# Differential values projected 512 columns wide, gates of two groups in every other stage

## The chip, the cores and the metric

The kernel runs on one core of a Trainium2 chip. The metric is the device time of one execution in microseconds (us); shorter is better.

## The reference, cut to what matters

Two layers (`DEPTH = 2`) over 512 frames of width 2048, all in float32. In each layer one input projection feeds three things: differential attention (8 heads, two softmax maps each), latent attention (8 heads, "MLA") and a SiLU gate. Then comes one output projection.

```python
for l in range(DEPTH):
    h = _rmsnorm(x, norm_g[l])
    proj = jnp.einsum('bsd,de->bse', h, w_in[l])
    dq, dk, dv, cq, ckv, kr, gate = jnp.split(proj, offs, axis=-1)
    ...
    o_a = _diff_attention(dq[:, :, 0], dq[:, :, 1], dk[:, :, 0], dk[:, :, 1], dv, lam, rel_bias)
    ...
    o_b = _mla_attention(q_nope, q_rope, k_nope, k_rope, v_b)
    ...
    y = jnp.concatenate([o_a, o_b], axis=-1) * jax.nn.silu(gate)
    x = x + jnp.einsum('bse,ed->bsd', y, w_out[l])
return _rmsnorm(x, final_norm_g)
```

The change touches `dv` (the values of the differential heads, 1024 columns of `w_in`), the first 1024 columns of `gate`, and where the values of both attentions are kept.

## The kernel before

**Weights.** They are read in units of at most 128 x 1024 elements (`in_units`, `plan`). `emit_dma` loads a unit to `raw`; `emit_split` makes of it a rounded part `whi` on ScalarE (L195) and a remainder `wlo` on VectorE (L196). Activations are kept as such pairs too. A product is three matmuls (`mm3`, L249): high by high, low by high, high by low. Four pairs of `whi` and `wlo` are in use at a time, and the split runs two units ahead of the unit in work.

**Groups.** `group` makes the pieces of one projection: for each unit, for each of `nb` output blocks, one piece. The outer loop is over units, so all `nb` blocks accumulate at once, each in a PSUM bank of its own, from a pool `pj` of four. When a block has had its last piece, `evac` copies it out, and the bank goes to the next group that asks. `mm_T` holds the weight still and streams 512 frames (moving operand 512 wide, output transposed); `mm_S` holds the activation still and streams the weight columns, so that its matmuls are as wide as the unit.

**Stages.** In each layer TensorE works through CQ (four blocks, `mm_S`, 512 wide), then four stages `i` = 0 to 3, one for each pair of differential heads, then a last stage with gates and CKV, then the output projection and MLA. Stage `i` has

- G (only from `i` = 1 on): the gates of pair `i-1`, 2 blocks, 4 units of 4 k-blocks, `mm_T`: pieces of 12 matmuls;
- V: the values of pair `i`, 4 blocks, 4 units of 4 k-blocks by 256 columns, `mm_S`: pieces of 12 matmuls, 256 wide;
- QK: queries and keys of pair `i`, 4 blocks, 8 units of 2 k-blocks, `mm_T`: pieces of 6 matmuls.

The last stage has G of pair 3, then the gates of MLA (GM, two groups of 4 blocks with pieces of 6 matmuls), then CKV.

**Evacuation.** The four blocks of QK are evacuated by `evac_qk`: blocks 0 and 1 (queries) take two copies on ScalarE and two subtractions on VectorE (L486) each; blocks 2 and 3 (keys) take four copies on ScalarE (L99) and four subtractions on VectorE (`kl`, L746) each, which read the bank until their end. A block of V takes one copy, on ScalarE or VectorE in turn (L751); a block of gates an exponential and a copy on ScalarE, while its reciprocals and its product (L719, L720, L724) are put into a list, `later`, that `run_later` spreads over the pieces that follow.

**Attention.** The attention of pair `i-1` is cut into items (`diff_items`): scores, softmax, transposes (L309), product with the values (L573), norm, and the product with the gate (L592). `mix` lays them between the pieces of stage `i` by the pieces' costs, from a share `MIX_DIFF` of the stage on to its end. So each engine's order is written out by the program; the engines meet by semaphores, and each works through its own list in order.

Of the kernel before, what the change touches and what calls it, by code (L numbers as in the profile page):

```python
# [11 lines left out]
F32 = mybir.dt.float32  # L12
# [5 lines left out]
P = 128  # L18
S = 512
NSB = S // P  # L20
# [21 lines left out]
MLAG = (0, 2, 3, 4)  # L42
PACE = 1.365
SQ_DVE = (0, 2)
EDGE = ((11, 13, 19, 21), (17, 23, 25, 28))
MIX_NORM = (-0.11, 0.63)
MIX_DIFF = (0.08, 1.0)
# [7 lines left out]
def tile_hybrid_trunk(ctx, tc, x, norm_g, w_in, diff_lambda, diff_subln_g, mla_q_norm_g,  # L55
                      mla_w_q_b, mla_kv_norm_g, mla_w_kv_b, w_out, rel_bias, final_norm_g,
                      onehot, cos2, sin1, out):
    nc = tc.nc
# [4 lines left out]
    def pool(name, bufs, space=None):  # L63
        kw = {} if space is None else {"space": space}
        return ctx.enter_context(tc.tile_pool(name=name, bufs=bufs, **kw))
# [3 lines left out]
    rawp = pool("raw", RAW)  # L69
    whip = pool("whi", BUFS)  # L70
    wlop = pool("wlo", BUFS)
    vp = pool("v", 2)
    smp = pool("sm", 4)
    ptp = pool("pt", 2)
    bip = pool("bias", 2)
# [10 lines left out]
    def B(shape, dtype, name):  # L86
        return big.tile(shape, dtype, tag="B", name=name)
# [20 lines left out]
    def in_units(l, cols, nk):  # L108
        w = sum(c for _, c in cols)
        ids = []  # L110
        for k0 in range(0, KD, nk):
            n = min(nk, KD - k0)
            srcs, off = [], 0
            for c0, cw in cols:
                srcs.append((off, cw, w_in[l, k0 * P:(k0 + n) * P, c0:c0 + cw].rearrange("(k p) c -> p k c", p=P)))
                off += cw
            ids.append((add_unit(srcs, n, w), k0, n))
        return ids
# [31 lines left out]
    for l in range(DEPTH):  # L150
        g = {}
        g["CQ"] = in_units(l, [(O_CQ, QL)], 2)
        for i in range(4):
            if i:
                g["G", i - 1] = in_units(l, [(O_GATE + (i - 1) * 256, 256)], 4)
            g["V", i] = in_units(l, [(O_DV + i * 256, 256)], 4)
            g["QK", i] = in_units(l, [(O_DQ + i * 256, 256), (O_DK + i * 256, 256)], 2)
        g["G", 3] = in_units(l, [(O_GATE + 3 * 256, 256)], 4)
        for c in range(2):
            g["GM", c] = in_units(l, [(O_GATE + 1024 + c * 512, 512)], 2)  # L160
        g["CKV"] = in_units(l, [(O_CKV, KVL + ROPE)], 3)
        g["OD", 0] = out_units(l, 0, 0)
        g["QR"] = qr_units(l)
        for j in range(4):
            g["QN", j] = qn_units(l, j)
            g["KV", j] = kv_units(l, j)
            if j:
                g["OD", j] = out_units(l, j, 0)
        for c in range(4):
            g["OM", c] = out_units(l, c, 8)  # L170
        plan.append(g)
# [145 lines left out]
    with tc.manual_schedule():  # L317
# [228 lines left out]
        def diff_items(l, i, qk, v, gate):  # L546
            slots = []
            for hp in range(2):
                h = 2 * i + hp
                o_ = {}  # L550
                for qb in range(NSB):
                    st_ = {}

                    def a(hp=hp, h=h, qb=qb, st_=st_, o_=o_):
                        if qb == 0:
                            if h not in biases:
                                biases[h] = load_bias(h)
                            o_["o"] = T("o", op, "o")
                            o_["ssq"] = stat("ssq")
                            o_["bt"] = biases.pop(h)  # L560
                        if qb == 1 and hp == 0:
                            biases[h + 1] = load_bias(h + 1)
                        diff_scores(l, qk[hp], qb, o_["bt"], st_)
                        if qb == NSB - 1:
                            qk.pop(hp)

                    def b(qb=qb, st_=st_):
                        transpose_p(qb, st_)

                    def c(hp=hp, qb=qb, o_=o_, st_=st_):  # L570
                        bk = bank("ov")
                        for kb in range(qb + 1):
                            nc.tensor.matmul(bk[:, :P], lhsT=st_["pt"][:, kb * P:(kb + 1) * P],  # L573
                                             rhs=v["t"][:, kb, hp * P:(hp + 1) * P], start=kb == 0, stop=kb == qb)
                        acopy(o_["o"][:, qb * P:(qb + 1) * P], bk[:, :P], scale=st_["rc"])
                        nc.scalar.activation(bk[:, :P], bk[:, :P], AF.Square, scale=st_["rc"],
                                             accum_out=o_["ssq"][:, qb:qb + 1])

                    slot = [a, b, c]
                    if qb == NSB - 1:  # L580
                        def d1(o_=o_):
                            rs = stat("ors")
                            rsqrt(rs[:, 0:4], o_["ssq"][:, 0:4], 4, 1.0 / (2 * DH))
                            o3 = o_["o"].rearrange("p (b d) -> p b d", b=NSB)
                            nc.vector.tensor_tensor(o3, o3, rs[:, 0:4].unsqueeze(2).to_broadcast([P, NSB, P]), op=ALU.mult)

                        def d2(h=h, o_=o_):
                            bk = bank("oT")
                            for b in range(NSB):
                                pe_t(bk[:, b * P:(b + 1) * P], o_["o"][:, b * P:(b + 1) * P])  # L590
                            y = gate(h)
                            nc.vector.scalar_tensor_tensor(out=y, in0=bk, scalar=gsub[:, l:l + 1], in1=y, op0=ALU.mult, op1=ALU.mult)  # L592

                        slot += [d1, d2]
                    slots.append(slot)
            return pipeline(slots, DLAG)

        def mla_items(l, j, qk, v, gate, rope):
            slots = []
            for hp in range(2):  # L600
                h = 2 * j + hp
                o_ = {}
                for qb in range(NSB):
                    st_ = {}

                    def a(hp=hp, qb=qb, st_=st_):
                        mla_scores(qk["t"], hp, j, rope, qb, st_)
                        if hp == 1 and qb == NSB - 1:
                            qk.pop("t")
                            if j % 2:  # L610
                                rope.pop(("q", j // 2))

                    def b(qb=qb, st_=st_):
                        transpose_p(qb, st_)

                    def c(hp=hp, qb=qb, o_=o_, st_=st_):
                        if qb == 0:
                            o_["bk"] = bank("oT")
                        for kb in range(qb + 1):
                            nc.tensor.matmul(o_["bk"][:, qb * P:(qb + 1) * P], lhsT=v["t"][:, kb, hp * P:(hp + 1) * P],  # L620
                                             rhs=st_["pt"][:, kb * P:(kb + 1) * P], start=kb == 0, stop=kb == qb)

                    slot = [a, b, c]
                    if qb == NSB - 1:
                        def d(h=h, o_=o_):
                            y = gate(h)
                            nc.vector.tensor_tensor(y, o_.pop("bk"), y, op=ALU.mult)

                        slot.append(d)
                    slots.append(slot)  # L630
            return pipeline(slots, MLAG)
# [9 lines left out]
        for l in range(DEPTH):  # L641
            g = plan[l]
            ah = act_h(l)
# [84 lines left out]

            pend = []
            for i in range(4):  # L730
                qk, v = {}, {}

                def evac_qk(b, bk, qk=qk):
                    if b < 2:
# [10 lines left out]
                        for n in (m, 1 - m):  # L745
                            nc.vector.tensor_tensor(hd["kl"][half(n), m], bk[half(m)], k[half(m), m].bitcast(F32), op=ALU.subtract)  # L746

                def evac_v(b, bk, v=v):
                    if "t" not in v:
                        v["t"] = vp.tile([P, NSB, 256], F32, tag="v", name="v")  # L750
                    (nc.vector.tensor_copy if b % 2 else acopy)(v["t"][:, b, :], bk[:, :256])  # L751

                pieces = []
                if i:
                    pieces += group(g["G", i - 1], 2, mm_T(ah), evac_gate(2 * i - 2))
                pieces += group(g["V", i], NSB, mm_S(ah, 256), evac_v, cost=2)
                pieces += group(g["QK", i], 4, mm_T(ah), evac_qk)
                mix(pieces, pend, MIX_DIFF)
                pend = diff_items(l, i, qk, v, gate_y)
# [7 lines left out]
                    split_pair(gates[h // 4][:, h % 4:h % 4 + 2, :], y[j])  # L767
                return item

            pieces = group(g["G", 3], 2, mm_T(ah), evac_gate(6))  # L770
            for c in range(2):
                pieces += group(g["GM", c], 4, mm_T(ah), evac_gate(8 + 4 * c))
            pieces += group(g["CKV"], NSB, mm_S(ah, KVL + ROPE), evac_ckv, cost=2.6)
# [123 lines left out]
            def mla_proj(j, qk, v):  # L897
# [16 lines left out]
                def kv_piece(b):  # L914
# [16 lines left out]
                    if sb == 3:  # L931
                        finish(u)
                    if "t" not in v:
                        v["t"] = vp.tile([P, NSB, 256], F32, tag="v", name="vm")
                    if sb % 2 == 1:
                        src = banks[0].rearrange("p (b c) -> p b c", b=2)
                        (nc.vector.tensor_copy if sb == 1 else acopy)(v["t"][:, sb - 1:sb + 1, :], src)

                return pieces + [(8 if b < 2 else 4, lambda b=b: kv_piece(b)) for b in range(6)]

            def out_pieces(key, y, evac, ahead=2):
                return group(g[key], NSB, mm_S(act_y(y), 512), evac, ahead=ahead)

            qkv = [({}, {}) for _ in range(4)]
            mix(mla_proj(0, *qkv[0]), even([lambda p=p: qr_T(p) for p in range(4)]), MIX_QR)
            gm = lambda h, gate_y=gate_y: gate_y(8 + h)
            pend = mla_items(l, 0, *qkv[0], gm, rope)
# [123 lines left out]
```

## Time and profile before

| | |
|---|---|
| median of 3 runs | 1766.7 us (1764.92 to 1767.01) |
| the profiled execution | 1766.37 us |
| its span, first to last instruction | 1764.6 us |
| TensorE (PE) busy | 1735.2 us, 98% of the span |
| VectorE (DVE) busy | 970.0 us, 55% |
| ScalarE (ACT) busy | 703.3 us, 40% |
| mean granted TensorE clock | 0.996 |

PE is the matmuls, PEld the loads of their stationary operands. A matmul's busy time reaches into the next one's, since they are pipelined: what one costs is the distance from its start to the next start, and not its own duration. A busy share of PE alone therefore doesn't tell that it runs at its peak.

### The profile page before, as it was taken

The page shows a single profiled execution, that of the slowest core. Times are in us where ns is not written, and L with a number is a line of the kernel's source. Part 1 is how long each engine was busy: PE and PEld are TensorE (multiplying, and loading weights), DVE is VectorE, ACT ScalarE, POOL GpSimd, SP SyncE. Part 2 cuts the span into 40 slices and gives each one's busy share as a digit, 9 for nine tenths or more (in the row PEclk, how much of TensorE's full clock was granted, in tenths as well). Part 3 has the DMA queues.
Part 4 walks back from the last instruction along what each step waited for, and adds up shares of the span by engine and source line. Part 5 has one row for each costly group of instructions (what it writes and reads, how often), then busy time and mean ns, then how long its engine had stood idle before and what let it go on. Part 6 is the DMA issues. An engine that isn't in the chain of part 4 may idle for free.

```text
span 1764.6 us, 23519 instructions
## 1 busy us (share of the span) xinstructions
PE 1735.2 (98%) x9245; PEld 1486.4 (84%) x9245; DVE 970.0 (55%) x1785; ACT 703.3 (40%) x1424; POOL 32.0 (2%) x53
## 2 busy tenths in 40 slices
PE   6999999999999999999999999999999999999997
PEld 4888889898888988888879898888988898888886
DVE  5425646463656774464362263654645676655554
ACT  5324434443443443333362244443543444433433
POOL 1000000000000000000000000000000000000000
PEclk9999999999999999999999999999999999999999
DMA  5552323232332432313333333332324225213223
GB/s 180 163 160 84 96 84 108 72 119 76 105 95 81 123 105 64 120 60 117 122 107 89 92 104 88 96 97 83 108 72 129 75 84 155 72 61 120 84 90 125
DMA packets 142330, 179.34 MB, mean 102 GB/s; under 512 B 16942, under 2 KB 94812, under 8 KB 142092
## 3 DMA queue, kind: packets, MB, share of 16 engines
q1 hardware_dynamic: 142220, 177.85, 33.0%
q8 instruction: 72, 1.18, 0.3%
q14 instruction: 38, 0.31, 0.1%
HBM read 169.39 MB, written 13.67 MB: 104 GB/s over the span
## 4 chain that ended last, share of the span: by engine, by line
PE 97%; ACT 1%; DVE 1%; DMA 1%; issue 0%; POOL 0%; SPq 0%; ACTq 0%; POOLq 0%; DVEq 0%
PE pj L249 84%; PE oT L620 2%; PE ov L573 2%; PE pT L309 2%; PE sc L523 2%; PE sc L493 2%; PE sc L492 2%; PE nT L309 1%; DMA xs<-in_x 1%; PE oT L309 0%; PE cT L309 0%; ACT xn L99 0%; DVE nt L457 0%; ACT whi L195 0%; ACT junk L424 0%
## 5 line engine op out<-in xcount | busy, mean ns | idle before, releaser
L196 DVE TENSOR_TENSOR wlo<-raw,whi 128x1024 fp32r<-128x1024 f32 (+1 forms) x272 | 327.5, 1211 | 298.1 <-ACT whi L195 291.9
L249 PE MATMUL pj<-hThi,whi 128*128 128x512 f32 x1024 | 410.0, 400 | 0.0
L249 PE MATMUL pj<-hThi,wlo 128*128 128x512 f32 x1024 | 400.3, 391 | 0.0
L249 PE MATMUL pj<-hTlo,whi 128*128 128x512 f32 x1024 | 399.3, 390 | 0.0
L195 ACT ACTIVATE whi<-raw 128x1024 fp32r<-128x1024 f32 (+1 forms) x272 | 282.7, 1047 | 182.2 <-PE pj L249 106.3
L249 PE MATMUL pj<-whi,yhl 128*128 128x512 f32 x1024 | 323.8, 397 | 0.0
L249 PE MATMUL pj<-whi,hThi 128*128 128x256 f32 (+2 forms) x768 | 241.4, 314 | 2.1 <-ACT hThi L99 2.1
L249 PE MATMUL pj<-whi,hTlo 128*128 128x256 f32 (+2 forms) x768 | 236.1, 307 | 0.0
L249 PE MATMUL pj<-wlo,hThi 128*128 128x256 f32 (+2 forms) x768 | 235.9, 307 | 0.0
L249 PEld LDWEIGHTS pj<-hThi,wlo 128*128 128x128 f32 x1024 | 192.2, 188 | 41.8
L249 PEld LDWEIGHTS pj<-hThi,whi 128*128 128x128 f32 x1024 | 192.7, 188 | 36.6
L249 PEld LDWEIGHTS pj<-hTlo,whi 128*128 128x128 f32 x1024 | 192.9, 188 | 35.6
L249 PEld LDWEIGHTS pj<-whi,yhl 128*128 128x128 f32 x1024 | 185.5, 188 | 34.0
L249 PE MATMUL pj<-wlo,yhl 128*128 128x512 f32 x512 | 200.6, 392 | 0.0
L509 ACT ACTIVATE s<-s,mx 128x128 f32<-128x128 f32 (+3 forms) x128 | 71.0, 555 | 300.5 <-DVE mx L507 300.5
L249 PEld LDWEIGHTS pj<-whi,hThi 128*128 128x128 f32 x768 | 147.4, 192 | 7.8 <-ACT hThi L99 2.5
L249 PEld LDWEIGHTS pj<-whi,hTlo 128*128 128x128 f32 x768 | 147.2, 192 | 5.7 <-DVE hTlo L462 0.7
L249 PEld LDWEIGHTS pj<-wlo,hThi 128*128 128x128 f32 x768 | 146.9, 191 | 5.4
L249 PEld LDWEIGHTS pj<-wlo,yhl 128*128 128x128 f32 x512 | 96.1, 188 | 21.3
L720 DVE RECIPROCAL ge<-ge 128x256 f32<-128x256 f32 x64 | 112.2, 1753 | 2.2
L503 DVE CUSTOM_DVE_ANT_0 s<-sc,bt 128x128 f32<-128x128 f32 (+3 forms) x128 | 57.1, 483 | 79.4 <-POOL bt L413 54.2
L529 ACT ACTIVATE s<-sc,mx 128x128 f32<-128x128 f32 (+1 forms) x64 | 33.8, 528 | 137.9 <-DVE mx L527 137.9
(153 smaller groups left out, 1870.2 us busy)
## 6 DMA issues: line engine op xcount, KB each, us to landing
raw<-in_w_in SPq DMA_DIRECT2D x112, 512.0 KB, 3.8
raw<-in_w_in SPq DMA_DIRECT2D x128, 256.0 KB, 3.0
raw<-in_w_out SPq DMA_DIRECT2D x64, 512.0 KB, 3.7
xs<-in_x SPq DMA_DIRECT2D x32, 256.0 KB, 5.4
bt<-btab SPq DMA_DIRECT2D x16, 512.0 KB, 5.2
btab<-vecd SPq DMA_DIRECT2D x16, 320.0 KB, 6.2
raw<-in_w_in SPq DMA_DIRECT2D x10, 480.0 KB, 3.7
raw<-in_mla_w_q_b SPq DMA_DIRECT2D x16, 256.0 KB, 3.4
```

Of the source, the lines that this page charges most:

```text
L195: nc.scalar.activation(hi[:, :n], raw[:, :n], AF.Copy)
L196: nc.vector.tensor_tensor(lo[:, :n], raw[:, :n], hi[:, :n].bitcast(F32), op=ALU.subtract)
L249: nc.tensor.matmul(dst, lhsT=a, rhs=b, start=first and t == 0, stop=last and t == 2)
L309: nc.tensor.transpose(dst, src, ident)
L492: nc.tensor.matmul(dst, lhsT=q[:, m], rhs=khi, start=first, stop=False)
L493: nc.tensor.matmul(dst, lhsT=q[:, m], rhs=klo, start=False, stop=True)
L503: nc.vector.tensor_tensor_reduce(out=sm_t[:, :w], in0=bk[:, :w], in1=bt[:, m, 512 - w:512], op0=ALU.add, op1=ALU.max, scale=1.0, scalar=LO ...
L509: nc.scalar.activation(s[m][:, :w], s[m][:, :w], AF.Exp, bias=mx[:, 2 + m:3 + m], accum_out=sm[:, m:m + 1])
L523: nc.tensor.matmul(bk[:, :w], lhsT=qk[:, par, q], rhs=qk[:, 2 + par, :w], start=True, stop=False)
L573: nc.tensor.matmul(bk[:, :P], lhsT=st_["pt"][:, kb * P:(kb + 1) * P], rhs=v["t"][:, kb, hp * P:(hp + 1) * P], start=kb == 0, stop=kb == qb)
L620: nc.tensor.matmul(o_["bk"][:, qb * P:(qb + 1) * P], lhsT=v["t"][:, kb, hp * P:(hp + 1) * P], rhs=st_["pt"][:, kb * P:(kb + 1) * P], start ...
L720: nc.vector.reciprocal(e[:, c], e[:, c])
```

## The change

Values of the differential heads are projected for two pairs of heads at once: the group V exists for `i` = 0 and 2 alone, 512 columns wide, with 8 units of 2 k-blocks. Each of its pieces has 6 matmuls of 512 columns, where before there were 12 of 256. The gates follow a table `GATES`: stage 1 computes the gates of pairs 0 and 1, stage 3 those of pairs 2 and 3, stages 0 and 2 none, and the last stage begins with GM. The tile of values is 128 x 4 x 512: the first of a layer in the pool `v`, which now has one buffer, the second in the pool of big tiles. The values of MLA are kept in one tile with two halves, used by `j % 2`.

```diff
+GATES = ((), (0, 1), (), (2, 3))
...
-    vp = pool("v", 2)
+    vp = pool("v", 1)
...
         for i in range(4):
-            if i:
-                g["G", i - 1] = in_units(l, [(O_GATE + (i - 1) * 256, 256)], 4)
-            g["V", i] = in_units(l, [(O_DV + i * 256, 256)], 4)
+            for n in GATES[i]:
+                g["G", n] = in_units(l, [(O_GATE + n * 256, 256)], 4)
+            if i % 2 == 0:
+                g["V", i] = in_units(l, [(O_DV + i * 256, 512)], 2)
             g["QK", i] = in_units(l, [(O_DQ + i * 256, 256), (O_DK + i * 256, 256)], 2)
-        g["G", 3] = in_units(l, [(O_GATE + 3 * 256, 256)], 4)
...
-                                             rhs=v["t"][:, kb, hp * P:(hp + 1) * P], start=kb == 0, stop=kb == qb)
+                                             rhs=v["t"][:, kb, h % 4 * P:(h % 4 + 1) * P], start=kb == 0, stop=kb == qb)
+                        if h % 4 == 3 and qb == NSB - 1:
+                            v.pop("t")
...
-                    (nc.vector.tensor_copy if b % 2 else acopy)(v["t"][:, b, :], bk[:, :256])
+                        v["t"] = B([P, NSB, 512], F32, "v") if i else vp.tile([P, NSB, 512], F32, tag="v", name="v")
+                    (nc.vector.tensor_copy if b % 2 else acopy)(v["t"][:, b, :], bk)
...
-                if i:
-                    pieces += group(g["G", i - 1], 2, mm_T(ah), evac_gate(2 * i - 2))
-                pieces += group(g["V", i], NSB, mm_S(ah, 256), evac_v, cost=2)
+                for n in GATES[i]:
+                    pieces += group(g["G", n], 2, mm_T(ah), evac_gate(2 * n))
+                if i % 2 == 0:
+                    pieces += group(g["V", i], NSB, mm_S(ah, 512), evac_v)
                 pieces += group(g["QK", i], 4, mm_T(ah), evac_qk)
...
-            pieces = group(g["G", 3], 2, mm_T(ah), evac_gate(6))
+            pieces = []
```

How the order of instructions moves is seen on PE at three places. Each row is an instruction: line, operation, what it writes and reads (with the tiles' numbers), size, and the engines whose semaphores it waits for. A `pj` tile is one block's bank; `oT` are transposes of the attention of the pair before.

The first place is the start of V in stage 0 of the first layer, after the last matmul of CQ. Before:

```order
L249 MATMUL pj_453<-wlo_614,hThi_410 128x512
L249 MATMUL pj_699<-whi_645,hThi_167 128x256 [waits Activation_49]
L249 MATMUL pj_699<-whi_645,hTlo_168 128x256
L249 MATMUL pj_699<-wlo_646,hThi_167 128x256 [waits DVE_49]
...
L249 MATMUL pj_712<-whi_645,hThi_167 128x256 [waits DVE_49]
```

And now:

```order
L250 MATMUL pj_453<-whi_613,hTlo_411 128x512
L250 MATMUL pj_453<-wlo_614,hThi_410 128x512
L250 MATMUL pj_698<-whi_645,hThi_167 128x512 [waits Activation_49]
L250 MATMUL pj_698<-whi_645,hTlo_168 128x512
L250 MATMUL pj_698<-wlo_646,hThi_167 128x512 [waits DVE_49]
...
L250 MATMUL pj_705<-whi_645,hThi_167 128x512 [waits DVE_49]
```

The matmuls are twice as wide; a piece has 6 of them in place of 12, so that the second block (`pj_712`, `pj_705`) comes after 6.

The second place is the step from stage 1 to stage 2, between the last piece of QK (`pj_1758` before, `pj_1692` now, block 3) and what follows. Before, G of pair 1 follows:

```order
L309 MATMUL oT_2088<-ident_110,o_1636 128x128 [waits Activation_49] x2
L249 MATMUL pj_1758<-hThi_410,whi_1962 128x512
...
L249 MATMUL pj_2115<-hThi_167,whi_2011 128x512 [waits DVE_49,PE_49,Activation_49]
...
L249 MATMUL pj_2128<-hThi_167,whi_2011 128x512 [waits DVE_49,PE_49]
...
L249 MATMUL pj_2115<-hThi_176,whi_2045 128x512 [waits Activation_49]
```

Now V of pairs 2 and 3 follows:

```order
L310 MATMUL oT_2025<-ident_110,o_1589 128x128 [waits Activation_49] x2
L250 MATMUL pj_1692<-hThi_410,whi_1899 128x512
...
L250 MATMUL pj_2052<-whi_1948,hThi_167 128x512 [waits DVE_49,PE_49,Activation_49]
...
L250 MATMUL pj_2059<-whi_1948,hThi_167 128x512 [waits DVE_49,PE_49]
...
L250 MATMUL pj_2066<-whi_1948,hThi_167 128x512 [waits DVE_49,PE_49]
...
L250 MATMUL pj_2073<-whi_1948,hThi_167 128x512 [waits DVE_49,PE_49]
...
L250 MATMUL pj_2052<-whi_1982,hThi_167 128x512 [waits Activation_49]
```

Before, the group after QK takes two banks, the second 12 matmuls after the first. Now it takes all four, one after each 6 matmuls, and each first matmul waits for VectorE.

The third place is the step from stage 3 to the last stage. Before, G of pair 3 follows QK (`pj_3569` is its block 3), on two banks:

```order
L249 MATMUL pj_3569<-hThi_410,whi_3773 128x512
L249 MATMUL pj_3569<-hTlo_411,whi_3773 128x512
...
L249 MATMUL pj_3926<-hThi_167,whi_3822 128x512 [waits DVE_49,PE_49,Activation_49]
...
L249 MATMUL pj_3939<-hThi_167,whi_3822 128x512 [waits DVE_49,PE_49]
...
L249 MATMUL pj_3926<-hThi_176,whi_3856 128x512 [waits Activation_49]
```

Now GM follows (`pj_3302` is block 3 of QK), on four banks:

```order
L250 MATMUL pj_3302<-hThi_410,whi_3509 128x512
...
L250 MATMUL pj_3662<-hThi_167,whi_3558 128x512 [waits DVE_49,PE_49,Activation_49]
...
L250 MATMUL pj_3669<-hThi_167,whi_3558 128x512 [waits DVE_49,PE_49]
...
L250 MATMUL pj_3676<-hThi_167,whi_3558 128x512 [waits DVE_49,PE_49]
...
L250 MATMUL pj_3683<-hThi_167,whi_3558 128x512 [waits DVE_49,PE_49]
```

Here too the four banks of QK are asked for 6 matmuls apart, by a group that stood behind another one before.

## Rows read from the trace of the kernel before

**Rows 1.** The page: shares of the chain that ended last.

```profile
PE 97%; ACT 1%; DVE 1%; DMA 1%; issue 0%; POOL 0%; SPq 0%; ACTq 0%; POOLq 0%; DVEq 0%
```

**Rows 2.** Waits of PE, all: who for whom, us in total, times, longest.

```profile
PE nT L309 <- ACT xn L99: 11.2, 8, 3.1
PE gbk L362 <- DMA gsrc<-in_diff_subln_g: 6.7, 1, 6.7
PE pj L249 <- ACT hThi L99: 2.1, 1, 2.1
```

**Rows 3.** Windows: two of V, then two of CQ.

```profile
core 0: us, PE busy (x) PEld busy (x) DVE busy (x) ACT busy (x) POOL busy (x), PEclk, DMA share, GB/s
76.39:99.42 23.03, 23.03 (x194) 23.03 (x193) 7.05 (x7) 6.13 (x8) 0.00 (x0) 1.00 0.83 246
943.78:966.82 23.04, 23.04 (x194) 23.03 (x193) 5.83 (x6) 5.08 (x7) 0.00 (x0) 1.00 0.30 93
916.49:943.78 27.29, 27.29 (x123) 22.61 (x121) 9.24 (x10) 8.10 (x10) 0.00 (x0) 1.00 0.42 116
59.93:76.39 16.46, 16.46 (x74) 13.63 (x74) 4.95 (x6) 3.97 (x6) 0.00 (x0) 1.00 0.70 217
```

**Rows 4.** Timeline of PE, stage 1 to 2: start us, us, instruction.

```profile
242.88 0.48 PE L249 MATMUL pj<-hThi,whi 128*128 128x512 f32 x1
...
244.36 0.40 PE L249 MATMUL pj<-hThi,whi 128*128 128x512 f32 x1
...
245.74 0.39 PE L249 MATMUL pj<-hThi,whi 128*128 128x512 f32 x1
...
247.10 0.39 PE L249 MATMUL pj<-hThi,whi 128*128 128x512 f32 x1
```

**Rows 5.** Timeline of DVE there (idle before it and its releaser in brackets).

```profile
241.23 2.81 DVE L486 SCALAR_TENSOR_TENSOR qk<-pj,qk 64x512 fp32r<-64x512 f32 x4 [2.02 <-ACT qk L99]
...
246.60 1.40 DVE L746 TENSOR_TENSOR kl<-pj,qk 64x512 fp32r<-64x512 f32 x2 [0.66 <-ACT qk L99]
248.03 0.75 DVE L592 SCALAR_TENSOR_TENSOR gate<-oT,gsub,gate 128x512 f32<-128x512 f32 x1
248.70 1.37 DVE L746 TENSOR_TENSOR kl<-pj,qk 64x512 fp32r<-64x512 f32 x2
250.74 1.40 DVE L746 TENSOR_TENSOR kl<-pj,qk 64x512 fp32r<-64x512 f32 x2 [0.66 <-ACT qk L99]
```

**Rows 6.** Timeline of DVE, stage 3 to the last one.

```profile
449.45 1.40 DVE L746 TENSOR_TENSOR kl<-pj,qk 64x512 fp32r<-64x512 f32 x2 [0.66 <-ACT qk L99]
...
453.58 1.40 DVE L746 TENSOR_TENSOR kl<-pj,qk 64x512 fp32r<-64x512 f32 x2 [0.66 <-ACT qk L99]
```

**Rows 7.** Timeline of ACT at the layers' boundary.

```profile
893.62 1.32 ACT L99 ACTIVATE xn<-xs,rs 128x512 f32<-128x512 f32 x2
```

**Rows 8.** Timeline of PE there.

```profile
894.38 1.73 PE L309 MATMUL nT<-ident,xn 128*128 128x128 f32 x8 [2.23 <-ACT xn L99]
...
896.77 0.63 PE L249 MATMUL pj<-wlo,hThi 128*128 128x512 f32 x1
897.19 0.63 PE L249 MATMUL pj<-whi,hThi 128*128 128x512 f32 x1
```

**Rows 9.** Windows there.

```profile
894.96:898.37 3.41, 3.41 (x11) 2.90 (x11) 2.69 (x5) 2.12 (x4) 0.00 (x0) 0.50 0.75 229
898.37:901.78 3.41, 3.41 (x20) 2.87 (x20) 2.52 (x3) 1.91 (x4) 0.00 (x0) 1.00 0.22 29
```

**Rows 10.** Windows: stage 1 from its first attention on, then stage 2.

```profile
153.84:244.36 90.52, 90.52 (x534) 80.01 (x533) 47.21 (x99) 37.68 (x91) 2.43 (x4) 1.00 0.35 105
244.36:345.79 101.43, 101.43 (x582) 89.05 (x581) 55.74 (x110) 42.81 (x99) 2.41 (x4) 1.00 0.32 94
```

**Rows 11.** The page: the costliest part of a gate.

```profile
L720 DVE RECIPROCAL ge<-ge 128x256 f32<-128x256 f32 x64 | 112.2, 1753 | 2.2
```

More of the change, by code (lines that the diff above doesn't have):

```diff
@@ L568, in b, with c @@
                         transpose_p(qb, st_)
-                    def c(hp=hp, qb=qb, o_=o_, st_=st_):
+                    def c(h=h, qb=qb, o_=o_, st_=st_):
                         bk = bank("ov")
@@ L619, in c @@
                         for kb in range(qb + 1):
-                            nc.tensor.matmul(o_["bk"][:, qb * P:(qb + 1) * P], lhsT=v["t"][:, kb, hp * P:(hp + 1) * P],
+                            nc.tensor.matmul(o_["bk"][:, qb * P:(qb + 1) * P], lhsT=v["t"][:, j % 2, kb, hp * P:(hp + 1) * P],
                                              rhs=st_["pt"][:, kb * P:(kb + 1) * P], start=kb == 0, stop=kb == qb)
@@ L730, in tile_hybrid_trunk @@
             for i in range(4):
-                qk, v = {}, {}
+                qk = {}
+                if i % 2 == 0:
+                    v = {}
                 def evac_qk(b, bk, qk=qk):
@@ L746, in evac_qk, with evac_v @@
                             nc.vector.tensor_tensor(hd["kl"][half(n), m], bk[half(m)], k[half(m), m].bitcast(F32), op=ALU.subtract)
-                def evac_v(b, bk, v=v):
+                def evac_v(b, bk, v=v, i=i):
                     if "t" not in v:
-                        v["t"] = vp.tile([P, NSB, 256], F32, tag="v", name="v")
-                    (nc.vector.tensor_copy if b % 2 else acopy)(v["t"][:, b, :], bk[:, :256])
+                        v["t"] = B([P, NSB, 512], F32, "v") if i else vp.tile([P, NSB, 512], F32, tag="v", name="v")
+                    (nc.vector.tensor_copy if b % 2 else acopy)(v["t"][:, b, :], bk)
                 pieces = []
-                if i:
-                    pieces += group(g["G", i - 1], 2, mm_T(ah), evac_gate(2 * i - 2))
-                pieces += group(g["V", i], NSB, mm_S(ah, 256), evac_v, cost=2)
+                for n in GATES[i]:
+                    pieces += group(g["G", n], 2, mm_T(ah), evac_gate(2 * n))
+                if i % 2 == 0:
+                    pieces += group(g["V", i], NSB, mm_S(ah, 512), evac_v)
                 pieces += group(g["QK", i], 4, mm_T(ah), evac_qk)
@@ L933, in kv_piece @@
                     if "t" not in v:
-                        v["t"] = vp.tile([P, NSB, 256], F32, tag="v", name="vm")
+                        v["t"] = vp.tile([P, 2, NSB, 256], F32, tag="v", name="vm")
                     if sb % 2 == 1:
                         src = banks[0].rearrange("p (b c) -> p b c", b=2)
-                        (nc.vector.tensor_copy if sb == 1 else acopy)(v["t"][:, sb - 1:sb + 1, :], src)
+                        (nc.vector.tensor_copy if sb == 1 else acopy)(v["t"][:, j % 2, sb - 1:sb + 1, :], src)
                 return pieces + [(8 if b < 2 else 4, lambda b=b: kv_piece(b)) for b in range(6)]
@@ L942, in out_pieces @@
                 return group(g[key], NSB, mm_S(act_y(y), 512), evac, ahead=ahead)
-            qkv = [({}, {}) for _ in range(4)]
+            vm = {}
+            qkv = [({}, vm) for _ in range(4)]
             mix(mla_proj(0, *qkv[0]), even([lambda p=p: qr_T(p) for p in range(4)]), MIX_QR)
```

## The prediction

> **What bounds the kernel now.** I read the chain of waits first. The reader is to see that 97% of it is PE [rows 1]: whatever PE spends less or more, the kernel spends less or more. Then the waits of PE: 20.0 us in all, every one at the first projection or at the boundary of the layers, none at a `pj` bank and none at an item of attention [rows 2]. So in the stages that the change touches PE never stood still, and two questions decide: what do PE's own instructions cost there, and does the new order make PE wait where it did not. The windows and the timelines answer them. Outside the span the profiled execution has 1766.37 - 1764.6 = 1.8 us, which nothing here touches; it stands 0.3 us below the median of the runs, so a sum against the one holds for the other.
>
> **Part 1, wider matmuls: a gain.** A V group before is 4 blocks x 16 k-blocks x 3 = 192 matmuls, 256 wide. The group that runs alone, without attention between its pieces, takes 23.03 us in the first layer and 23.04 us in the second [rows 3]: 120 ns from start to start. (The counts in these rows include two or three that reach over an edge; the counts here are those of the program.) A matmul of the new kind, 512 columns with the activation held still, already runs in CQ: 120 of them in 27.29 us and 72 in 16.46 us [rows 3], 227 to 229 ns. One new matmul replaces two old ones, so a group of 192 becomes 96: 96 x 0.2274 = 21.8 us or 96 x 0.2286 = 21.9 us. The gain is 1.1 to 1.2 us a group; with 4 pairs in 2 layers, 8 groups, 8.7 to 9.6 us. I take 9.1 us.
>
> The Trainium skill, TensorE: Matmul & The Clock Gate, section "Back-to-back issue gap", gives for an isolated matmul a start-to-start gap of its columns over 2.4 GHz plus 2.5 ns. As an estimate by that rule a 256 wide one is 109.2 ns and a 512 wide one 215.8 ns, so that 768 replacements would bring 768 x 2.6 ns = 2.0 us and not 9.1. The trace doesn't agree with it here, at 120 and 227 ns. By that rule the forecast below would be 7.1 us higher.
>
> **Part 2, QK's banks: a new wait.** This is the part that the diff hides. Before, each QK was followed by a G group, which needs two banks and stays in them for 96 matmuls; V came 22 us later. Now QK of stage 1 is followed at once by V, and QK of stage 3 by GM; both want all four banks within 18 matmuls. (QK of stages 0 and 2 still meets a G group.) So in each layer there are two such steps, four in all. The pool hands the banks out in turn, so block b of the new group takes the bank of QK's block b.
>
> What QK's evacuation takes stands in the trace, since it is the same before. At the step from stage 1 to stage 2 the last block of QK starts at 242.88 us, and the group behind it at 244.36 us, its seventh matmul at 245.74, its thirteenth at 247.10 [rows 4]; in the new order these are the starts of blocks 0, 1 and 2. The evacuation is a chain of ScalarE copies and VectorE subtractions that goes block by block [rows 5]:
>
> - blocks 0 and 1 are read for the last time at the latest at 241.23 + 2.81 = 244.04 us, before they are wanted: no wait;
> - block 2 is read until 246.60 + 1.40 = 248.00 us, and wanted at 247.10;
> - then a product of the attention goes in between (L592, 248.03 to 248.78), and block 3 is read until 250.74 + 1.40 = 252.14 us, and would be wanted at 247.10 + 1.37 = 248.47.
>
> From the end of an instruction that PE waits for to PE's start I take 0.05 us: the first of two `xn`, 1.32 us together, ends a little after the half of it, 894.3, and PE, which waits for it, goes on at 894.38 [rows 7, 8]. So block 2 starts at 248.05, 0.95 us late; its six matmuls end the due time of block 3 at 249.42, and it starts at 252.19, 2.77 us late. Together 3.72 us of PE standing still. From stage 3 to the last stage the chain has the same distances: 453.58 + 1.40 = 454.98, which is 4.13 us after block 2's 450.85 [rows 6], as 252.14 after 248.00. Four steps cost 14.9 us.
>
> Nothing hides this: PE works in order, so behind the waiting matmul stand the rest of V (or GM), then the first scores of the next attention, and the engines behind PE wait for those. What the wait gives DVE and ACT, a few us to catch up, is worth nothing, since PE doesn't wait for them afterwards. Bounds of the term: at the least, blocks 2 and 3 are wanted later by some transposes or scores that fall between the pieces, or the chain is shorter by the L592 that stands in it (0.7 us a step), 12 us; at the most, the chain begins later by one weight split in front of it, about 1.2 us a step, 20 us. I take the middle reading, 14.9, because the instructions in the chain and their order are the same in the new program.
>
> **Part 3, the clock after the wait: a further loss, uncertain.** The trace has one stop of PE of this length in full work: 2.23 us, until 894.38 [rows 8]. Soon after it the granted clock is 0.50 from 894.96 to 898.37 [rows 9], that is 1.2 in place of 2.4 GHz; matmuls start 0.42 us apart there (896.77, 897.19 [rows 8]). In 3.41 us PE does then what takes 3.41 x 0.2274 / 0.427 = 1.82 us at the full clock: 1.6 us lost. The new stops, 0.95 us, 1.37 us of work, 2.77 us, are longer in the second part and broken in the first, so each may or may not cost this. Bounds: none of four, 0, and all four, 6.4 us. I take two of four, 3.2 us.
>
> **Edits at no cost, and their cover.** The copies of V are half as many and twice as wide, one a block; between the end of a block and the next use of its bank by QK there are 18 matmuls as before, 4.1 us, and such steps never held PE [rows 2]. Gates move: stages 1 and 3 have four blocks in place of two, stages 2 and the last one two fewer. A block of gates costs DVE two reciprocals of 1.75 us [rows 11] and some 1.2 us besides, about 5 us, so 10 us more in a stage whose DVE is busy 55.74 of 101.43 us [rows 10]. There is room; where a burst made one softmax late, PE would lose a us or so in stages 1 and 3, up to 3 us in all, which I keep for the upper end. Each gate is ready no later than before for the head that needs it. The loads stay 512 KB per unit in the same number, in rows twice as long, at a DMA share of 0.30 to 0.35 in the stages [rows 10]. The big tiles have one more in use; as a stage releases two and takes two, a slot is free each time. The one buffer of values is written by MLA long after the first heads have read it.
>
> **Sum.** 1766.4 - 9.1 + 14.9 + 3.2 = 1775.4 us, slower by 0.5%.
>
> **The rivals.**
>
> - *No wait at the banks.* If QK's blocks came free in time, the gain alone would be left: 1766.4 - 9.1 = 1757.3 us. For it speaks that PE never waited for a bank where four blocks follow four (CQ to V, V to QK, GM to GM) [rows 2]. Against it: none of those evacuates with eight operations a block, and QK's, which does, ended 8 us after QK in the trace. 8%.
> - *Half a wait.* Only the second stop counts, and for less, because transposes fall in between or DVE has less in its way: some 8 us in place of 14.9 and the full clock throughout, 1766.4 - 9.1 + 8 = 1765.3 us, no change that can be told. 8%.
> - *The wait, and the full clock.* The stops are too short or too broken to bring the clock down: 1766.4 - 9.1 + 14.9 = 1772.2 us. For it speaks that the work of block 2 lies between the two stops; against it, that 2.77 us is more than the 2.23 us that did it once. 24%.
> - *The wait, all four drops, and late softmaxes behind them.* 1766.4 - 9.1 + 14.9 + 6.4 = 1778.6 us, and up to 3 us more for the bursts of gates, 1781.6 us. 12%.
> - *The wide matmul saves only the isolated gap's 2 us.* This needs 768 wide matmuls to run slower, or V's 256 wide ones to have been held up, neither of which the windows show: 1766.4 - 2 + 14.9 + 3.2 = 1782.5 us. 1%.
>
> The forecast itself, one to three drops of the clock, has 47%, from 1766.4 - 9.1 + 14.9 + 1.6 = 1773.8 to 1777.0 us.
>
> **How the numbers follow.** About 0.2%, 3.5 us, is what a measurement of this kernel can tell from no change: faster is below 1763.2, slower above 1770.2. Faster is the first rival, 8%; the same is the second, 8%; the rest, 84%, is slower. The range leaves the first two out below and about 4% above: 1770 to 1781 us.
>
> **What would show it.** In the profile after: V's matmuls, 768 of them at 512 wide, 227 ns apart; in the waits of PE a line of `pj` waiting for DVE's `kl` (L751 there), eight times, some 15 us in total, the longest about 2.8 us, at the steps from stage 1 to 2 and from stage 3 to the last one in both layers, and none from stage 0 to 1 or 2 to 3; and a granted clock of 0.5 for 3.4 us behind some of them. The prediction is wrong if PE shows no such waits, or if the chain of QK's evacuation ends earlier against QK's last matmul than the 7.8 us (244.36 to 252.14) of the trace before.

## The result, and the profile after

The changed kernel takes 1778.15 us (median of 4 runs, 1776.9 to 1778.86), the kernel before 1766.56 (1764.92 to 1767.01) beside it: ratio 1.0063, 95% interval 1.0051 to 1.0076. It is slower, by 11.6 us. The profiled execution took 1778.14 us, its span is 1776.4, 11.8 more than before.

The chain that ended last, shares by engine; before, PE alone had 97% [rows 1]:

```profile
PE 93%; DVE 2%; ACT 2%; DMA 1%; issue 1%; POOL 0%; SPq 0%; ACTq 0%; POOLq 0%; DVEq 0%
```

The waits of PE, all of them (us in total, times, longest). The first line is new; the other three answer to [rows 2]:

```profile
PE pj L250 <- DVE kl L751: 13.6, 8, 2.5
PE nT L310 <- ACT xn L100: 10.3, 8, 2.4
PE gbk L363 <- DMA gsrc<-in_mla_q_norm_g: 7.1, 1, 7.1
PE pj L250 <- ACT hThi L100: 2.1, 1, 2.1
```

The step from stage 1 to stage 2 on PE, then one line of the step from stage 3 to the last stage:

```profile
266.99 0.39 PE L250 MATMUL pj<-wlo,hThi 128*128 128x512 f32 x1
268.27 0.47 PE L250 MATMUL pj<-whi,hThi 128*128 128x512 f32 x1 [0.89 <-DVE kl L751]
268.57 0.39 PE L250 MATMUL pj<-whi,hTlo 128*128 128x512 f32 x1
...
269.50 0.40 PE L250 MATMUL pj<-wlo,hThi 128*128 128x512 f32 x1
272.40 0.64 PE L250 MATMUL pj<-whi,hThi 128*128 128x512 f32 x1 [2.51 <-DVE kl L751]
272.83 0.63 PE L250 MATMUL pj<-whi,hTlo 128*128 128x512 f32 x1
...
478.91 0.47 PE L250 MATMUL pj<-hThi,whi 128*128 128x512 f32 x1 [2.52 <-DVE kl L751]
```

And VectorE there, to be laid beside [rows 5]:

```profile
266.72 1.40 DVE L751 TENSOR_TENSOR kl<-pj,qk 64x512 fp32r<-64x512 f32 x2 [0.66 <-ACT qk L100]
268.15 0.75 DVE L595 SCALAR_TENSOR_TENSOR gate<-oT,gsub,gate 128x512 f32<-128x512 f32 x1
268.82 1.37 DVE L751 TENSOR_TENSOR kl<-pj,qk 64x512 fp32r<-64x512 f32 x2
270.85 1.40 DVE L751 TENSOR_TENSOR kl<-pj,qk 64x512 fp32r<-64x512 f32 x2 [0.66 <-ACT qk L100]
```

The `kl` that reads block 2 ends at 266.72 + 1.40 = 268.12, and PE starts block 2 at 268.27; the one that reads block 3 ends at 272.25, and PE starts block 3 at 272.40. So PE starts 0.15 us after the read, and not 0.05. The number in brackets counts from a modelled end: from start to start the stops are 268.27 - 266.99 = 1.28 and 272.40 - 269.50 = 2.90 us, where 0.23 is usual, so 1.05 and 2.67 us. The second matmul after a stop starts 0.30 us after the first in place of 0.23 (268.27, 268.57), which adds 0.08 for each stop. A step costs 3.88 us, four cost 15.5.

Windows of the changed kernel: behind the second stop in stage 2, behind the second stop in the last stage, and a V group that runs alone:

```profile
core 0: us, PE busy (x) PEld busy (x) DVE busy (x) ACT busy (x) POOL busy (x), PEclk, DMA share, GB/s
...
272.55:275.96 3.41, 3.41 (x9) 2.67 (x10) 2.10 (x2) 0.16 (x1) 0.00 (x0) 0.50 0.35 80
478.91:482.32 3.41, 3.41 (x15) 2.82 (x16) 2.24 (x2) 0.31 (x1) 0.00 (x0) 1.00 0.33 74
949.35:992.90 43.55, 43.55 (x194) 36.05 (x193) 11.01 (x10) 9.48 (x11) 0.00 (x0) 1.00 0.33 97
```

The granted clock is 0.50 behind two of the four steps (from stage 1 to 2, in both layers) and 1.00 behind the other two. The V group alone takes 43.55 us where two groups of 256 took 2 x 23.04 [rows 3].

**Where the 11.8 us come from.** All distances between starts on PE, summed by kind of matmul: the 1536 matmuls of 256 columns (187.3 us) are gone, and those of 512 columns with the activation held still take 187.7 us more. In the 187.7 are two steps of stops (7.8) and two stretches at half the clock (1.6 each, 3.2), so that without them the wide values save 10.6 us. The 512-column matmuls with the weight held still take 10.5 us more; the two other steps are 7.8 of it. Of the last 2.7 some 1.7 lie with the matmuls that are first after an instruction of the attention: their median is 0.31 us in place of 0.23, and 196 of them have the weight held still where there were 172. That goes with the order of the groups and not with the width: the kernel with the values first, below, has its matmuls as wide as before, and shows 196 of them and 2.9 us more. The net gain is about 7.9 us. -7.9 + 15.5 + 3.2 = 10.8; the program's start and end take 0.4 (a DMA) and 0.2 us more, and 0.3 is spread over the other kinds, which makes the 11.8 up to rounding.

### The profile page after: what moved, and what is told of

It is laid out like the page before. It is cut to its first block, busy times and chain, and to the rows that moved or that the text cites. A ratio compares the mean times of both kernels' runs of the same rounds, so it can differ in the third digit from the quotient of the medians.

```text
span 1776.4 us, 21979 instructions
## 1 busy us (share of the span) xinstructions
PE 1733.5 (98%) x8477; PEld 1447.2 (81%) x8477; DVE 969.2 (55%) x1777; ACT 702.8 (40%) x1416; POOL 32.1 (2%) x53
## 4 chain that ended last, share of the span: by engine, by line
PE 93%; DVE 2%; ACT 2%; DMA 1%; issue 1%; POOL 0%; SPq 0%; ACTq 0%; POOLq 0%; DVEq 0%
PE pj L250 80%; PE oT L623 2%; PE ov L574 2%; PE pT L310 2%; PE sc L524 2%; PE sc L494 2%; PE sc L493 2%; DVE kl L751 1%; ACT qk L100 1%; PE nT L310 1%; DMA xs<-in_x 1%; DMA bt<-btab 0%; PE oT L310 0%; PE cT L310 0%; ACT xn L100 0%
## 5 line engine op out<-in xcount | busy, mean ns | idle before, releaser
L250 PE MATMUL pj<-whi,hThi 128*128 128x512 f32 (+1 forms) x512 | 196.7, 384 | 8.9 <-DVE kl L751 6.8
L250 PE MATMUL pj<-whi,hTlo 128*128 128x512 f32 (+1 forms) x512 | 192.9, 377 | 0.0
L250 PE MATMUL pj<-wlo,hThi 128*128 128x512 f32 (+1 forms) x512 | 192.5, 376 | 0.0
L250 PEld LDWEIGHTS pj<-whi,hThi 128*128 128x128 f32 x512 | 98.1, 192 | 25.4 <-issue 8.6
L250 PEld LDWEIGHTS pj<-wlo,hThi 128*128 128x128 f32 x512 | 98.2, 192 | 16.3
L250 PEld LDWEIGHTS pj<-whi,hTlo 128*128 128x128 f32 x512 | 98.1, 192 | 14.9 <-DVE hTlo L463 0.7
```

The costliest lines, as they stand in the source:

```text
L250: nc.tensor.matmul(dst, lhsT=a, rhs=b, start=first and t == 0, stop=last and t == 2)
```

## The experiments

All runs were timed against the kernel before on the same chip, in five rounds. Theory A is the prediction's: wide values gain, and PE's stops at QK's banks, with the clock behind them, lose more. Theory B: the gates, moved to other stages, cost the time. Theory C: wide values gain next to nothing.

**The changed kernel again**, without an edit.

> The changed kernel once more, beside the three others. Theory A (banks): the loss is four steps at which PE stands still until QK's banks are free (3.9 us each from start to start in its profile, 15.5 us in all) and a lower clock behind some of them (1.6 us each), against a gain of about 9 us from wide values: 1778 us, 11.6 us above the kernel before, with one to four drops of the clock at these steps. Theory B (gates): the loss comes with the moved gates, whose work bursts in stages 1 and 3. Theory C (wide values): wide matmuls gain nothing here. All three expect 1777 to 1779 us of this run.

Measured: 1777.52 us (1774.78 to 1778.67) against 1766.93, ratio 1.0056, interval 1.0043 to 1.0069. PE waited for `kl` 13.6 us in 8 times again, and the clock was 0.50 behind the same two steps.

**QK between the gates.** In stages 1 and 3 the second group of gates goes behind QK, so that QK always meets a group on two banks. 

```diff
...
-                for n in GATES[i]:
+                for n in GATES[i][:1]:
                     pieces += group(g["G", n], 2, mm_T(ah), evac_gate(2 * n))
                 if i % 2 == 0:
                     pieces += group(g["V", i], NSB, mm_S(ah, 512), evac_v)
                 pieces += group(g["QK", i], 4, mm_T(ah), evac_qk)
+                for n in GATES[i][1:]:
+                    pieces += group(g["G", n], 2, mm_T(ah), evac_gate(2 * n))
```

> Stages 1 and 3 compute the same two groups of gates, but QK stands between them and not behind them, so that a group that takes two banks follows each QK. Theory A: no wait of PE for kl, no new drop of the clock in the stages, and the gain of the wide values alone is left: 1766.6 - 9.1 = 1757.5 us, 1756 to 1759. Theory B: the gates are still moved, 1774 to 1779 us. Theory C: without a gain, 1766 us or more.

Measured: 1759.99 us (1759.69 to 1761.1), ratio 0.9961, interval 0.9948 to 0.9973: faster than both kernels, 17.5 us below the changed one in the same job. PE's waits, complete:

```profile
PE nT L312 <- ACT xn L100: 10.3, 7, 3.1
PE gbk L365 <- DMA gsrc<-in_diff_subln_g: 8.2, 1, 8.2
PE pj L252 <- ACT hThi L100: 2.1, 1, 2.1
```

No stop at a bank is left, and the clock stays at 1.00 in the stages. Gates, values and widths are those of the change; only the group behind QK is another. So B and C fall, and A stands. The time lies 1 us above its range: in the trace the wide values save 10.7 us, but 1.8 come back on the matmuls with the weight held still, 1.2 on the attention's products with the values and 0.7 in small parts, so that 7.0 are left and not 9.

**Blocks 2 and 3 later.** The group behind QK does blocks 0 and 1 of its first three units before it asks for banks 2 and 3.

```diff
+LATE = [(i, b) for pr in ((0, 1), (2, 3)) for i in range(3) for b in pr] + [(i, b) for i in range(3, 8) for b in range(4)]
...
-                    pieces += group(g["V", i], NSB, mm_S(ah, 512), evac_v)
+                    pieces += group(g["V", i], NSB, mm_S(ah, 512), evac_v, LATE if i else None)
...
-                pieces += group(g["GM", c], 4, mm_T(ah), evac_gate(8 + 4 * c))
+                pieces += group(g["GM", c], 4, mm_T(ah), evac_gate(8 + 4 * c), None if c else LATE)
```

> The changed order of groups stays, but V of stage 2 and the first group of MLA's gates work on blocks 0 and 1 for three units before they begin blocks 2 and 3, so that QK's last two banks are wanted 8.2 and 9.6 us after QK's end and not 2.7 and 4.1. Theory A: waits of PE for kl gone (they are free 3.7 and 7.8 us after it), 1757.5 us, 1756 to 1760. Theory B: nothing about the gates changes, 1777 to 1779 us. Theory C: 1766 us or more.

Measured: 1775.81 us (1774.16 to 1779.47), ratio 1.005, interval 1.0037 to 1.0064. The expectation missed. The waits for `kl` are gone, but two others stand there, four times each:

```profile
PE pj L251 <- ACT whi L197: 6.8, 4, 1.7
...
PE pj L251 <- DVE wlo L198: 4.0, 4, 1.0
```

The timelines of ACT and DVE at the step from stage 1 to 2 show why:

```profile
270.25 0.59 ACT L101 ACTIVATE qk<-pj 64x512 fp32r<-64x512 f32 x1 [1.69 <-DVE kl L752]
270.75 1.99 ACT L197 ACTIVATE whi<-raw 128x1024 fp32r<-128x1024 f32 x2
```

```profile
270.88 1.40 DVE L752 TENSOR_TENSOR kl<-pj,qk 64x512 fp32r<-64x512 f32 x2 [0.66 <-ACT qk L101]
272.31 2.36 DVE L198 TENSOR_TENSOR wlo<-raw,whi 128x1024 fp32r<-128x1024 f32 x2
```

The split of the next weights stands behind QK's evacuation on both engines. The new order takes up the second and third unit after 12 and 24 matmuls in place of 24 and 48, and so asks for splits before the evacuation lets them through. The banks were one thing that the evacuation holds up; the split is another. From start to start the new stops take 1.86 and 1.17 us a step, 12.1 in four, and the clock is 0.50 behind two of the steps, for 10.2 us in all: that is where the gain of the empty banks went.

**The stops filled.** Ahead of blocks 2 and 3, where PE stands still, 4 and 11 matmuls that nobody reads go into a bank of another pool. They add work only.

```diff
+                    for _ in range(n):
+                        nc.tensor.matmul(fb["t"], lhsT=a[:, 0, :P], rhs=a[:, 0, :], start=True, stop=True)
...
+                for k, n in ((1, 4), (2, 11)):
+                    pieces[k] = (pieces[k][0], after(pieces[k][1], n))
```

> The changed kernel with matmuls of no use in the stops: 4 ahead of block 2 and 11 ahead of block 3 of the group behind QK, 512 wide, 0.91 and 2.51 us, a little less than the stops of 1.05 and 2.67 us. Theory A: PE's idle time on kl falls below 0.3 us a step, no drop of the clock at these steps, and the time falls by the drops that the changed kernel has, two of four on average: 1778.2 - 3.3 = 1775 us, 1773 to 1776.5. If the lower clock costs nothing: 1778 us. If the matmuls come on top of the waits: 1778 + 4 x 3.4 = 1792 us.

Measured: 1773.82 us (1773.08 to 1774.86), ratio 1.0038, interval 1.0025 to 1.005; 3.7 us below the changed kernel. 60 matmuls more, 14.9 us of PE from start to start, make the kernel faster: the stops were time in which PE had nothing else to do. On PE, at the step from stage 1 to 2:

```profile
266.83 0.39 PE L250 MATMUL pj<-wlo,hThi 128*128 128x512 f32 x1
267.06 1.07 PE L740 MATMUL fill<-hThi 128*128 128x512 f32 x4
268.11 0.47 PE L250 MATMUL pj<-whi,hThi 128*128 128x512 f32 x1
...
269.34 0.39 PE L250 MATMUL pj<-wlo,hThi 128*128 128x512 f32 x1
269.57 2.68 PE L740 MATMUL fill<-hThi 128*128 128x512 f32 x11
272.24 0.47 PE L250 MATMUL pj<-whi,hThi 128*128 128x512 f32 x1
```

Blocks 2 and 3 start 1.28 and 2.90 us after the last matmul of the block ahead, exactly as in the changed kernel; the fill takes the place of the stop and adds nothing. The wait for `kl` is gone from the list, and the clock is full around the step:

```profile
core 0: us, PE busy (x) PEld busy (x) DVE busy (x) ACT busy (x) POOL busy (x), PEclk, DMA share, GB/s
266.00:276.00 10.00, 10.00 (x44) 7.66 (x43) 7.16 (x9) 4.80 (x7) 0.00 (x0) 1.00 0.15 37
```

Three stretches at half the clock are gone, those behind the two steps, 1.6 us each, and the one at the layers' boundary. That one costs 0.8 and not 1.6, since without it PE comes to the next `xn` too soon and waits for it: from the last matmul ahead of the boundary's wait to V it is 51.9 us with it and 51.1 without. Together 4.0 us; 3.7 measured. Since the steps are as long as before, this shows that the clock has a price of its own beside the stops.

**Values ahead of the gates, in the kernel before.** No wide values and no moved gates: in stages 1 to 3 V changes places with G, so that V follows QK in three steps of each layer.

```diff
...
-                if i:
-                    pieces += group(g["G", i - 1], 2, mm_T(ah), evac_gate(2 * i - 2))
                 pieces += group(g["V", i], NSB, mm_S(ah, 256), evac_v, cost=2)
+                if i:
+                    pieces += group(g["G", i - 1], 2, mm_T(ah), evac_gate(2 * i - 2))
```

> The kernel before, with one swap: in stages 1, 2 and 3 the values go ahead of the gates, so that QK of stages 0, 1 and 2 is followed at once by the values (256 wide, four banks, a bank every 12 x 0.12 = 1.44 us). Nothing else moves; QK of stage 3 still meets gates. Six such steps. Theory A (stops at QK's banks): PE waits for kl at six steps, twice in each; block 2 wanted 2.88 us after the group's start and free 3.69 after it, block 3 1.44 us after block 2 and free 4.13 us after it: 0.8 + 2.7 + 0.1 of restarts = 3.6 us a step, 21.6 in six, and 1.6 us for each drop of the clock, none to six: 1788 to 1798 us, 1793 with three. Theory C (it is the wide values that are held up, not the bank order): 1766 to 1769. Theory D (the copies that free the banks come earlier when the group behind is narrow): 1775 or less.

Measured: 1793.95 us (1792.25 to 1795.13) against 1767.35, ratio 1.0151, interval 1.0137 to 1.0165. This is the cleanest form of the loss: one swap in the old kernel makes it 26.6 us slower.

```profile
PE pj L249 <- DVE kl L746: 19.7, 12, 2.5
```

Twelve waits in six steps; from start to start 3.5 to 3.8 us a step, 21.7 in all, and the clock falls to 0.50 behind two of them. C and D, as this run's expectation has them (the wide values are held up; narrow ones free the banks sooner), fall.

**The gates put back.** Wide values, but one group of gates a stage, ahead of V, as before (`GATES = ((), (0,), (1,), (2,))`, and G of pair 3 at the head of the last stage).

> Values stay 512 wide for two pairs at once; the gates go back to one pair a stage, ahead of the values, so that QK is always followed by a group on two banks, as before. Theory A (stops at QK's banks): no wait of PE for kl, no drop of the clock in the stages, and the gain of the wide values alone; the sum said 9.1 us, the kernel with QK between the gates gave 6.9: 1757 to 1760 us. Theory B (the moved gates cost something of their own): lower than the kernel with QK between the gates (1760.0) by 1.5 us or more, 1758.5 or less. Theory C (the wide values gain next to nothing): 1764 to 1767.

Measured: 1800.75 us (1799.11 to 1801.83) against 1766.63, ratio 1.0192, interval 1.0178 to 1.0206. No theory had this: 40 us off, the wrong way. There is no wait for `kl`; the new ones are

```profile
PE pT L311 <- DVE s L515: 21.8, 4, 5.6
...
PE oT L311 <- DVE o L589: 8.6, 4, 2.2
...
PE pj L251 <- ACT gate L100: 1.3, 2, 0.6
```

Those of the first two lines lie in stages 1 and 3. TensorE's order of projections is the very one of the kernel with QK between the gates (G of pair 0, QK, G of pair 1, V, QK, ...). What differs is where a stage ends: `mix` lays the attention of a pair over G and QK alone here, 96 + 192 matmuls at 0.2275 us, some 66 us, and over two G and QK there, 384 matmuls, some 87 us. In stage 1, PE, then POOL (the last step of a bias tile's load):

```profile
171.87 0.22 PE L494 MATMUL sc<-qk 128*128 128x128 f32 x1
...
178.07 0.39 PE L251 MATMUL pj<-hThi,wlo 128*128 128x512 f32 x1
184.10 0.48 PE L311 MATMUL pT<-ident,s 128*128 128x128 f32 x1 [5.64 <-DVE s L515]
```

```profile
181.34 0.20 POOL L415 MEMSET bt<- 64x128 f32 x1 [147.95 <-DMA bt<-btab]
```

SyncE, which issues the loads, here and then in the kernel before:

```profile
172.99 2.01 SPq L184 DMA_DIRECT2D raw<-in_w_in  x4
175.05 0.97 SPq L412 DMA_DIRECT2D bt<-btab  x2
...
153.78 0.50 SPq L410 DMA_DIRECT2D bt<-btab  x1
```

The first transposes are wanted 6.4 us after the first scores; in the kernel before they came 9.2 us after them (153.84 and 163.00), with the bias there at 159.73. Now the bias comes at 181.34, softmax follows, and PE stands still for 5.8 us. Two things add up here. The transposes are wanted 2.8 us sooner after the scores; and the bias comes 9.5 us after them in place of 5.9, since its load is issued 3.2 us after the first scores, behind four loads of weights, and not with them, as in the kernel before. It is 3.2 us in all four stages. So more than half of the stop is the late load, and why the load is late is not shown. The window behind the stop:

```profile
184.10:188.30 4.20, 4.20 (x11) 3.33 (x12) 2.90 (x9) 2.32 (x6) 0.00 (x0) 0.50 0.03 6
```

The stops of this kernel are 33 us from start to start (22.5 ahead of `pT`, 9.3 ahead of `oT`, 1.6 at the evacuation of a gate). The half clock behind four of them takes some 8 more, an estimate from 16.7 us of work there at 0.427 us a matmul in place of 0.2275. That is the 41 us by which the run lies above the one with QK between the gates. So this run gives B no support; it goes the opposite way. The moved gates fill the stages that no longer have values, 87 us in each stage. How much of the 41 us is the short stage and how much the late load is open; that the bias's load alone would mend it was not tried.

**Narrow values in the new order.** The changed order and gates, but values 256 wide in every stage (against the changed kernel, cut to what matters).

```diff
...
-            if i % 2 == 0:
-                g["V", i] = in_units(l, [(O_DV + i * 256, 512)], 2)
+            g["V", i] = in_units(l, [(O_DV + i * 256, 256)], 4)
...
-                if i % 2 == 0:
-                    pieces += group(g["V", i], NSB, mm_S(ah, 512), evac_v)
+                pieces += group(g["V", i], NSB, mm_S(ah, 256), evac_v, cost=2)
```

> The order of the change (gates of two pairs in stages 1 and 3, none ahead of stage 2 and of the last groups), but values 256 wide for one pair in every stage. Theory A: the same four steps with four banks wanted at once, about 15 us of stops and 0 to 6.4 us of lower clock, without the gain of the wide values: 1766.9 + 15.2 + 3.2 = 1785.3, between 1781 and 1789. If stops and width simply add up, it lies as far above the changed kernel (1777.5) as the kernel before lies above the one with the gates put back. Theory C (the stops come from the wide values, whose pieces have half as many matmuls): 1766 to 1769. No clock loss at all: 1782.

Measured: 1797.84 us (1795.2 to 1798.64), ratio 1.0175, interval 1.0161 to 1.0189; 9 us above A's range.

```profile
PE pj L249 <- DVE kl L746: 14.1, 8, 2.2
...
PE oT L309 <- DVE o L585: 4.3, 2, 2.1
PE pT L309 <- DVE s L513: 3.2, 4, 1.3
```

The eight stops at the banks are there without wide values, 15.4 us from start to start, with two falls of the clock, 3.2. C, here that the stops come from the wide values, falls. The rest is again a short stage: stage 2 has V and QK alone, some 67 us, and PE waits there, and in stage 1, for the attention, some 8 us by the last two lines. Some 4 us stay unexplained; as a test of width against order this run is spoilt by its own uneven stages, and so is the sum that its expectation offered.

## Why the prediction was right

1776.9 to 1778.86 us lie within 1770 to 1781, and the forecast's mechanism is what the runs show. The sum itself, 1775.4, is 2.7 us low: 1.2 by the gain, 0.6 by the stops, 0.6 by the program's start and end, 0.3 in small parts. By the number alone the rival with four drops of the clock, 1778.6, lies nearer; that the trace has two drops and no late softmax decides against it. By the prediction's steps:

- **What bounds the kernel:** right. PE's own instructions and its waits account for the difference.
- **Part 1, the gain.** 9.1 us forecast, 7.9 measured. The wide values themselves save 10.6: 226.8 ns in the V group that runs alone (43.55 / 192), a little less than CQ showed. What was left out is the 2.7 us that come back on the matmuls with the weight held still, for the most part where the attention's instructions cut in. By the Trainium skill, TensorE: Matmul & The Clock Gate, section "Back-to-back issue gap", the isolated gap would have given 2 us; the trace doesn't agree with it, at 10.6.
- **Part 2, the stops.** 14.9 us forecast, 15.5 measured; single stops 0.95 and 2.77, measured 1.05 and 2.67. The chain of the evacuation was the same as before to 0.02 us (268.12 to 272.25 against 248.00 to 252.14). The 0.05 us from the read's end to PE is 0.15, which lengthens the first stop; the second is shorter because the six matmuls of block 2 took 1.46 us (268.27 to 269.73) and not 1.37. The slower second matmul, 0.08 behind each stop, was not counted. The places were right: eight waits, from stage 1 to 2 and from stage 3 to the last one. The rivals without a wait, or with half of one, fall.
- **Part 3, the clock.** 3.2 us forecast for two of four, two of four measured, 1.6 us each. The rival with the full clock falls. That it would be half of them was a guess; it came true by luck, and why just these two is open. The price was worked out at the layers' boundary, where a run without the fall shows that 0.8 us is saved; at the steps, where nothing else holds PE up, 1.6 holds.
- **Edits at no cost.** Right for this kernel: in its profile PE waits for no softmax (in that of its second run once, 0.3 us). But the prediction saw in the moved gates only a burden that had cover. That stages 1 and 3 would starve without them it did not see, and neither did the expectation of the run with the gates put back.
- **Not in the sum:** 0.6 us at the program's start and end, 0.4 of it a DMA there (7.1 against 6.7 us).

## What to carry to other kernels

When a group of work is moved behind another, ask which banks it wants first, and when the last reader of the group in front lets them go: a kernel in which PE never waited for a bank lost 26.6 us by one swap of two groups. The same evacuation also holds up whatever is queued behind it on its engines, so that a reordering which spares the banks may meet the weight split instead. Where one kind of work is laid between the pieces of another, what each stage has to offer as cover is a quantity to keep level; a change that empties a stage needs one that fills it.

## What the runs showed of the hardware

- A stop doesn't decide the clock by its length. 2.67 us brought it to 0.50 behind the steps into stage 2 and left it at 1.00 behind those into the last stage; of six such steps in the kernel with the values first, two were followed by 0.50. With the stops filled, even the fall at the layers' boundary [rows 9] was absent, though PE waited there as before.
- After a stop the second matmul starts 0.30 us after the first in place of 0.23, at the full clock.
- From the end of VectorE's read of a bank to the start of the matmul that waits for it there are 0.15 us.
- 60 useless matmuls in the stops made the kernel 3.7 us faster.
